# Column sums, mask loads and first small loads of the first product, in a two-block transformer kernel

## The chip, the cores and the metric

The kernel runs on one core of a Trainium2 chip. Times are device microseconds of one execution. The core's engines are TensorE (PE in the profile, its weight loads PEld), VectorE (DVE), ScalarE (ACT), GpSimd (POOL) and SyncE (SP, which issues nearly all DMAs here). Each engine takes its own instructions in order; an instruction waits for what it needs from the others.

## The reference

Two blocks of two layers each, for 256 rows of 1024 numbers, in float32. Only the start of the first layer matters here: an adaptive norm (adaLN), then the first product.

```python
def adaln_norm(x, c, g, w_ada, b_ada):
    mod = jax.nn.silu(c) @ w_ada + b_ada          # c: 1 x 1024, w_ada: 1024 x 3072
    shift, scale, gate = jnp.split(mod, 3, axis=-1)
    h = rms_norm(x, g) * (1.0 + scale[:, None, :]) + shift[:, None, :]
    return h, gate[:, None, :]

def nsa_mixer(h, w_in, pe_k, pe_v, ck_w1, ck_w2, cv_w1, cv_w2, w_out):
    u = h @ w_in                                   # the first product, 1024 x 2864
    ...                                            # q, k, v, z, gates are cut from u
    k_cmp = compress(k_c, pe_k, ck_w1, ck_w2)      # silu(blk @ w1) @ w2
    v_cmp = compress(v_c, pe_v, cv_w1, cv_w2)
    ...                                            # three attention branches, gated and projected
```

## The kernel before

Every large product is made in three matmuls of split float32 weights and activations: `make` (L199) loads one unit of a weight into one of five `wraw` buffers, ACT copies it to the high part (L210), and DVE subtracts to get the low part (L211). `pump` (L214) calls `make` as long as units are free. The five `wraw` buffers are shared by the weights of w_in and by those of adaLN.

The first product runs over the eight blocks k of 128 rows of w_in. For block k, `load` (L708) fetches the 128 shift and 128 scale columns of adaLN's weight, all 1024 rows, as two raw buffers `u` of four row blocks each, 1 MB in all, and two units of w_in (816 and 512 columns). `modulate(k)` (L720) forms, on 128 partitions, the sum over the eight row blocks r[j] times silu(c): ACT starts two accumulators ac (L725), DVE adds the other six row blocks in turn to one and to the other (L727), and PE sums each over the partitions against a column of ones (L731, L732; a float32 matmul is two instructions in the trace). From the sums come scale and shift (L734, L735), with which ACT makes block k of the normed input (L737, L740) and DVE its low part (L741). `multiply(k)` (L743) then adds block k to six accumulators in PSUM (L239, L240, L243). `modulate(k)` stands ahead of `multiply(k - 1)`, with a raised priority (`first(HEAD)`).

The order on each engine is set when the kernel is built, from priorities and from the order in which the program asks for things. After `modulate(7)` the program asks for the constants `cc` behind the last load so far, calls `pump` (the first four units of w_in's remaining 512 columns and two of the key compression's `nsa_ck_w1`), asks for the masks (`load_masks`, L159: two DMAs of 544 columns to 128 partitions into `wide` buffers, casts to bf16 on POOL), for the position table `peT` and the compression's second weights, and then for `multiply(7)`. Behind it come the copies of the product's results (`q_side`, `k_side`, `kvT`), the rope on DVE with its last addition on POOL (L440 to L442, L447), transposes on PE (L320), the rest of the product (`dense_cols`) and the compression (L839). `wide` has five buffers, taken in turn by xn, xn, m, m, then four q tiles (L810, filled at L812).

At the very start SP issues, in this order, the identity, the two halves of x, and three small columns `ccol`, `gcol`, `bcol` (8, 8 and 16 numbers to a partition), and then adaLN's first weights. [L127 to L137 below]

Of the kernel before, what the change touches and what calls it, by code (L numbers as in the profile page):

```python
# [8 lines left out]
F32 = mybir.dt.float32  # L9
F32R = mybir.dt.float32r  # L10
BF = mybir.dt.bfloat16
AF = mybir.ActivationFunctionType
ALU = mybir.AluOpType
# [81 lines left out]
def body(ctx: ExitStack, tc: tile.TileContext, A: dict, out: bass.AP, stop=None):  # L95
    nc = tc.nc
    pe, act, dve, pool = nc.tensor, nc.scalar, nc.vector, nc.gpsimd
# [8 lines left out]
    def nm(s):  # L106
        count[0] += 1
        return f"{s}{count[0]}"
# [11 lines left out]
    def ps(kind):  # L120
        b = banks[kind]
        i = turn.get(kind, 0)
        turn[kind] = i + 1
        return pp.tile([128, 512], F32, tag=f"b{b[i % len(b)]}", name=nm("ps"))


    ident = cp.tile([128, 128], F32, name="ident")  # L127
    nc.sync.dma_start(ident, A["k_ident"])
    x = [ap_.tile([128, D], F32, name=f"x{b}") for b in range(2)]
    for b in range(2):  # L130
        nc.sync.dma_start(x[b], A["x"][0, b * 128:(b + 1) * 128, :])
    ccol = cp.tile([128, 8], F32, name="ccol")
    nc.sync.dma_start(ccol, A["c_col"])
    gcol = cp.tile([128, 8], F32, name="gcol")
    nc.sync.dma_start(gcol, A["g_col"])
    bcol = cp.tile([128, 16], F32, name="bcol")
    nc.sync.dma_start(bcol, A["b_col"])  # L137
    ones = cp.tile([128, 128], F32, name="ones")
    dve.memset(ones, 1.0)
    nhalf = cp.tile([128, 1], F32, name="nhalf")  # L140
# [7 lines left out]
    def wide(name):  # L148
        return ap_.tile([128, D], F32, tag="bc", bufs=5, name=nm(name))
# [6 lines left out]
    def small(n=8):  # L156
        return ap_.tile([128, 12], F32, tag="sm", bufs=12, name=nm("sm"))[:, :n]

    def load_masks():  # L159
        for a, b in ((0, 544), (544, 1088)):  # L160
            m = wide("m")[:, :b - a]
            nc.sync.dma_start(m, A["k_mask"][:, a:b])
            if a == 0:
                pool.tensor_copy(mask[:, a:b], m)
            else:
                pool.tensor_copy(mask[:, a:1024], m[:, :1024 - a])
                pool.tensor_copy(mask[:, 1472:1536], m[:, 1024 - a:])
        pool.memset(mask[:, 1024:1152], 0.0)
        pool.tensor_copy(mask[:, 1152:1280], mask[:, 128:256])
        pool.memset(mask[:, 1280:1472], 0.0)  # L170

    def opened(name):
        cm = tc.tile_pool(name=name, bufs=1)
        return cm, cm.__enter__()

    def closed(cm):
        cm.__exit__(None, None, None)
# [3 lines left out]
    state = {"next": 0, "live": 0, "gate": None, "hold": False, "group": 2, "av": None}  # L181

    def behind(ins):
        return nullcontext() if ins is None else tc.issue_after(ins.ins)
# [29 lines left out]
    def pump():  # L214
        while not state["hold"] and len(made) < len(specs) and len(made) - (state["next"] - state["live"]) < NB:
            make()
# [11 lines left out]
    def mm3(p, xt, k, w, kw, c, start, stop):  # L228
        products(p, [(xt, k, w, kw)], c, start, stop)
# [107 lines left out]
    def rms_rstd(src, n, eps=1e-6):  # L337
        s = small(1)
        act.activation(junk[:, :n], src, AF.Square, accum_out=s)
        return rstd_of(s, 1.0 / n, eps)  # L340
# [278 lines left out]
    cs = cp.tile([128, 8], F32, name="cs")  # L619
# [77 lines left out]
    cmA, a0 = opened("ada0")  # L697
    xnT = a0.tile([128, 8, 256], F32, name="xnT")
    for tok in range(2):
        r = rms_rstd(x[tok], D)  # L700
# [19 lines left out]

    def modulate(k):
        r = raws[k]
        ac = [a0.tile([128, 256], F32, tag="aacc", bufs=4, name=nm("ac")) for _ in range(2)]
        for i in range(2):
            act.activation(ac[i], r[i], AF.Copy, scale=cs[:, i:i + 1])  # L725
        for j in range(2, 8):
            dve.scalar_tensor_tensor(ac[j % 2], r[j], cs[:, j:j + 1], ac[j % 2], op0=ALU.mult, op1=ALU.add)  # L727
        p = ps("pt")
        for i in range(2):
            c = slice(i * 128, (i + 1) * 128)  # L730
            pe.matmul(p[:, i:i + 1], lhsT=ac[0][:, c], rhs=ones[:, 0:1], start=True, stop=False)  # L731
            pe.matmul(p[:, i:i + 1], lhsT=ac[1][:, c], rhs=ones[:, 0:1], start=False, stop=True)  # L732
        ab = small(2)
        dve.scalar_tensor_tensor(ab[:, 1:2], p[:, 1:2], bcol[:, 8 + k:9 + k], gcol[:, k:k + 1], op0=ALU.add, op1=ALU.mult)  # L734
        dve.tensor_scalar(ab[:, 0:1], p[:, 0:1], bcol[:, k:k + 1], None, op0=ALU.add)  # L735
        hk = a0.tile([128, 256], F32, tag="hk", bufs=2, name=nm("hk"))
        act.activation(hk, xnT[:, k, :], AF.Identity, scale=ab[:, 1:2], bias=ab[:, 0:1])  # L737
        for tok in range(2):
            c = slice(tok * 128, (tok + 1) * 128)
            act.activation(xt[tok][0][:, k, :], hk[:, c], AF.Copy)  # L740
            dve.tensor_sub(xt[tok][1][:, k, :], hk[:, c], xt[tok][0][:, k, :].bitcast(F32))  # L741

    def multiply(k):  # L743
        state["next"] += 2
        w = made[state["next"] - 2:state["next"]]
        for gi, (i, c) in enumerate(((0, slice(0, 384)), (0, slice(384, 816)), (1, slice(0, 512)))):
            for tok in range(2):
                mm3(accp[gi * 2 + tok][:, :c.stop - c.start], xt[tok], k, w[i], 0, c, k == 0, k == 7)

    load(0)  # L750
    for k in range(8):
        if k < 7:
            load(k + 1)
        else:
            make()
            make()
        with first(HEAD):
            modulate(k)
        if k:
            multiply(k - 1)  # L760
# [1 line left out]
    with behind(state["dma"]):  # L762
        nc.sync.dma_start(cc, A["k_cc"])
    pump()
    load_masks()
    nc.sync.dma_start(peT, A["pe_T"])
    for j in range(2):
        nc.sync.dma_start(w2k[:, :, j * 64:(j + 1) * 64], A["nsa_ck_w2"][0].rearrange("(k p) n -> p k n", p=128))
    nc.sync.dma_start(w2v, A["nsa_cv_w2"][0].rearrange("(k p) n -> p k n", p=128))
    multiply(7)  # L770
    closed(cmA)


# [4 lines left out]
    with first(ATTN):  # L778
        pool.tensor_copy(cmask, cc[:, C_CADD:C_CADD + 2 * NCMP].rearrange("p (t n) -> p t n", t=2))
        for tok in range(2):  # L780
            dup = pK.tile([128, 4, 2, 64], F32, tag="kvd", bufs=2, name=nm("kvd"))
            act.activation(dup, accp[tok][:, :256].rearrange("p (a d) -> p a d", a=4)[:, :, None, :].to_broadcast([128, 4, 2, 64]), AF.Copy)
            p = ps("pt")
# [33 lines left out]
    with first(SINK):  # L817
        for tok in range(2):
            q_side(tok, 1, accp[4 + tok])
        for tok in range(2):  # L820
            k_side(accp[tok], tok, 256, 384, 0)
            p = accp[2 + tok]
# [30 lines left out]
    p = ps("c")  # L853
# [9 lines left out]
    for g in range(2):  # L863
        p = ps("c")
# [120 lines left out]
    with tc.tile_pool(name="dil", bufs=1) as dp:  # L985
# [42 lines left out]
        with first(ATTN):  # L1028
# [8 lines left out]
            for tok in range(2):  # L1037
# [10 lines left out]
                for i, (a, b) in enumerate(((0, 6), (6, 8))):  # L1048
                    c = slice(a * 64, b * 64)
# [118 lines left out]
    with tc.tile_pool(name="ab", bufs=1) as bp:  # L1168
# [74 lines left out]
        with first(ATTN):  # L1243
            o = [ps("o"), ps("o")]
            dve.tensor_scalar(nsink, sinks, -1.0, None, op0=ALU.mult)
            for h in range(8):
# [5 lines left out]
                if h % 2:  # L1252
                    c = slice(h - 1, h + 1)
# [153 lines left out]
```

## Time and profile before

| | us |
|---|---|
| median of 3 runs | 997.05 |
| lowest and highest | 995.78, 997.25 |
| the profiled execution's own time | 994.04 |
| its span, first to last instruction | 992.3 |
| PE busy in it | 934.9 (94%) |
| DVE busy | 701.5 (71%) |
| ACT busy | 538.8 (54%) |
| POOL busy | 40.6 (4%) |
| DMA, mean over the span | 179 GB/s |
| mean granted TensorE clock | 0.983 |

The shares are means over some thousand microseconds, most of which are feed-forward products. The first 80 us look different, and the change lies there. A timeline row gives the start, the length, the engine, the line and the operation; in brackets stands how long the engine sat idle before it, and what released it. A row of several instructions (x2) gives the time from the first one's start to the last one's end.

### The profile page before, as it was taken

The page shows a single profiled execution, that of the slowest core. Times are in us where ns is not written, and L with a number is a line of the kernel's source. Part 1 is how long each engine was busy: PE and PEld are TensorE (multiplying, and loading weights), DVE is VectorE, ACT ScalarE, POOL GpSimd, SP SyncE. Part 2 cuts the span into 40 slices and gives each one's busy share as a digit, 9 for nine tenths or more (in the row PEclk, how much of TensorE's full clock was granted, in tenths as well). Part 3 has the DMA queues.
Part 4 walks back from the last instruction along what each step waited for, and adds up shares of the span by engine and source line. Part 5 has one row for each costly group of instructions (what it writes and reads, how often), then busy time and mean ns, then how long its engine had stood idle before and what let it go on. Part 6 is the DMA issues. An engine that isn't in the chain of part 4 may idle for free.

```text
span 992.3 us, 14766 instructions
## 1 busy us (share of the span) xinstructions
PE 934.9 (94%) x5316; PEld 783.7 (79%) x5316; DVE 701.5 (71%) x1454; ACT 538.8 (54%) x1062; POOL 40.6 (4%) x49
## 2 busy tenths in 40 slices
PE   5997998899999998999799999999999899999996
PEld 4876786687778877967788888887997688888885
DVE  5888899858777768586857565677466676665655
ACT  5584567834545626486346554435676355555540
POOL 1003000001120001000000000000000000000000
PEclk9998798999999999999999999999999999999999
DMA  9996787334855425632356554655635243565541
GB/s 288 304 311 217 221 269 253 108 106 151 261 202 182 149 66 197 236 111 86 95 203 212 170 184 159 241 181 151 221 132 152 90 167 126 193 235 170 182 137 43
DMA packets 106169, 177.66 MB, mean 179 GB/s; under 512 B 8816, under 2 KB 40688, under 8 KB 106096
## 3 DMA queue, kind: packets, MB, share of 16 engines
q1 hardware_dynamic: 106096, 176.72, 54.6%
q8 instruction: 42, 0.69, 0.3%
q14 instruction: 31, 0.25, 0.1%
HBM read 175.65 MB, written 1.05 MB: 178 GB/s over the span
## 4 chain that ended last, share of the span: by engine, by line
PE 77%; DVE 11%; ACT 5%; DMA 4%; issue 2%; SPq 1%; POOL 0%; DVEq 0%; ACTq 0%; POOLq 0%
PE ps L279 15%; PE ps L239 13%; PE ps L240 13%; PE ps L243 13%; PE ps L280 8%; DVE wl L211 2%; DMA wr<-in_ada_w_dram 2%; PE ps L469 2%; PE ps L320 1%; DVE ac L660 1%; PE ps L839 1%; PE ps L525 1%; ACT e L482 1%; PE ps L297 1%; PE ps L298 1%
## 5 line engine op out<-in xcount | busy, mean ns | idle before, releaser
L211 DVE TENSOR_TENSOR wl<-wr,wh 128x1024 fp32r<-128x1024 f32 (+5 forms) x276 | 319.6, 1195 | 78.7 <-ACT wh L210 77.3
L210 ACT ACTIVATE wh<-wr 128x1024 fp32r<-128x1024 f32 (+5 forms) x276 | 270.6, 1021 | 72.4 <-PE ps L243 21.2
L279 PE MATMUL ps<-xhl,wh 128*128 128x512 f32 x640 | 226.5, 398 | 0.0
L239 PE MATMUL ps<-wh,xhl 128*128 128x512 f32 (+5 forms) x544 | 197.4, 375 | 4.5 <-ACT xhl L312 2.4
L240 PE MATMUL ps<-wl,xhl 128*128 128x512 f32 (+5 forms) x544 | 199.0, 368 | 0.0
L280 PE MATMUL ps<-xhl,wl 128*128 128x256 f32 x640 | 179.2, 281 | 0.0
L243 PE MATMUL ps<-wh,xhl 128*128 128x512 f32 (+5 forms) x544 | 172.9, 370 | 0.9 <-DVE xhl L313 0.6
L279 PEld LDWEIGHTS ps<-xhl,wh 128*128 128x128 f32 x640 | 120.0, 188 | 28.9
L280 PEld LDWEIGHTS ps<-xhl,wl 128*128 128x128 f32 x640 | 120.9, 189 | 1.1
L239 PEld LDWEIGHTS ps<-wh,xhl 128*128 128x128 f32 x544 | 103.6, 192 | 22.8 <-ACT xhl L312 5.1
L240 PEld LDWEIGHTS ps<-wl,xhl 128*128 128x128 f32 x544 | 104.5, 192 | 14.0 <-issue 0.2
L243 PEld LDWEIGHTS ps<-wh,xhl 128*128 128x128 f32 x544 | 99.8, 190 | 18.2 <-DVE xhl L313 2.4
L1124 ACT ACTIVATE hs<-ps 128x256 f32<-128x256 f32 x80 | 30.0, 377 | 100.1 <-PE ps L280 100.1
L1125 DVE TENSOR_TENSOR hs<-ps,hs 128x256 f32<-128x256 f32 x80 | 32.6, 420 | 68.4 <-ACT hs L1124 68.4
L243 PE MATMUL ps<-wh,hl 128*128 128x512 f32 x176 | 68.3, 390 | 0.0
L240 PE MATMUL ps<-wl,hh 128*128 128x512 f32 x176 | 68.3, 390 | 0.0
L239 PE MATMUL ps<-wh,hh 128*128 128x512 f32 x176 | 66.7, 390 | 0.0
L482 ACT ACTIVATE e<-e,sm 128x128 f32<-128x128 f32 x112 | 49.6, 445 | 12.7 <-DVE sm L476 12.6
L312 ACT ACTIVATE xhl<-ps 128x512 fp32r<-128x512 f32 x28 | 16.5, 597 | 67.9 <-PE ps L309 67.8
L476 DVE CUSTOM_DVE_ANT_0 e<-ps,mask 128x128 f32<-128x128 f32 (+1 forms) x144 | 44.1, 350 | 8.8 <-PE ps L489 4.3
L660 DVE SCALAR_TENSOR_TENSOR ac<-ar,cs,ac 128x512 f32<-128x512 f32 x56 | 42.7, 764 | 4.0 <-DMA ar<-in_ada_w_dram 3.7
L334 POOL TENSOR_TENSOR sm<-sm,nhalf 128x1 f32<-128x1 f32 x18 | 13.2, 734 | 721.3 <-DVE sm L333 721.3
(315 smaller groups left out, 1299.3 us busy)
## 6 DMA issues: line engine op xcount, KB each, us to landing
wr<-in_ffn_w_gate_dram SPq DMA_DIRECT2D x44, 512.0 KB, 4.7
wr<-in_ffn_w_up_dram SPq DMA_DIRECT2D x44, 512.0 KB, 4.7
wr<-in_ffn_w_down_dram SPq DMA_DIRECT2D x44, 512.0 KB, 5.0
ar<-in_ada_w_dram SPq DMA_DIRECT2D x32, 512.0 KB, 4.5
wr<-in_dil_w_in_dram SPq DMA_DIRECT2D x32, 512.0 KB, 4.6
wr<-in_cd_w_in_dram SPq DMA_DIRECT2D x22, 512.0 KB, 4.4
wr<-in_ada_w_dram SPq DMA_DIRECT2D x32, 256.0 KB, 4.9
wr<-in_nsa_w_in_dram SPq DMA_DIRECT2D x12, 512.0 KB, 5.0
```

The costliest lines, as they stand in the source:

```text
L210: act.activation(hi, raw[:, :nk * n], AF.Copy)
L211: dve.tensor_sub(lo, raw[:, :nk * n], hi.bitcast(F32))
L239: pe.matmul(p, lhsT=xt[0][:, k, :], rhs=w[0][:, kw, c], start=start and t == 0, stop=False)
L240: pe.matmul(p, lhsT=xt[0][:, k, :], rhs=w[1][:, kw, c], start=False, stop=False)
L243: pe.matmul(p, lhsT=xt[1][:, k, :], rhs=w[0][:, kw, c], start=False, stop=stop and t == n - 1)
L279: pe.matmul(p, lhsT=w[0], rhs=xhl[:, k].rearrange("p a t -> p (a t)"), start=k == 0, stop=False)
L280: pe.matmul(p[:, :256], lhsT=w[1], rhs=xh[:, k, :], start=False, stop=k == 7)
L476: state["dve"] = dve.tensor_tensor_reduce(out=e[:, c0:c1], in0=s[:, c0:c1], in1=added[:, 256 - (c1 - c0):], scale=-scale, scalar=3e38, op0 ...
L482: act.activation(e[:, c0:c1], e[:, c0:c1], AF.Exp, bias=n2[:, i:i + 1], scale=-1.0, accum_out=den[:, i:i + 1])
L660: dve.scalar_tensor_tensor(ac, raw[:, j, :], cs[:, k:k + 1], ac, op0=ALU.mult, op1=ALU.add)
L1124: act.activation(t[:, c], p[:, 256:], AF.Copy)
L1125: dve.tensor_add(t[:, c], p[:, :256], t[:, c])
```

## The change

Four edits. The identity and the three columns are issued from ACT's queue and no longer from SP's. `modulate` has one accumulator: ACT starts it with r[0], DVE adds seven row blocks one after the other into the same tile, and PE makes one sum over partitions for each of the two columns, where it made two. `load_masks` moves from ahead of `peT` and the small weights to behind `multiply(7)`, and it is bound to come behind the last weight load that `pump` has asked for, the second unit of `nsa_ck_w1`.

```diff
     ident = cp.tile([128, 128], F32, name="ident")
-    nc.sync.dma_start(ident, A["k_ident"])
+    nc.scalar.dma_start(ident, A["k_ident"])
...
-    nc.sync.dma_start(ccol, A["c_col"])
+    nc.scalar.dma_start(ccol, A["c_col"])
...
-    nc.sync.dma_start(gcol, A["g_col"])
+    nc.scalar.dma_start(gcol, A["g_col"])
...
-    nc.sync.dma_start(bcol, A["b_col"])
+    nc.scalar.dma_start(bcol, A["b_col"])
...
     def modulate(k):
         r = raws[k]
-        ac = [a0.tile([128, 256], F32, tag="aacc", bufs=4, name=nm("ac")) for _ in range(2)]
-        for i in range(2):
-            act.activation(ac[i], r[i], AF.Copy, scale=cs[:, i:i + 1])
-        for j in range(2, 8):
-            dve.scalar_tensor_tensor(ac[j % 2], r[j], cs[:, j:j + 1], ac[j % 2], op0=ALU.mult, op1=ALU.add)
+        ac = a0.tile([128, 256], F32, tag="aacc", bufs=4, name=nm("ac"))
+        act.activation(ac, r[0], AF.Copy, scale=cs[:, 0:1])
+        for j in range(1, 8):
+            dve.scalar_tensor_tensor(ac, r[j], cs[:, j:j + 1], ac, op0=ALU.mult, op1=ALU.add)
         p = ps("pt")
         for i in range(2):
             c = slice(i * 128, (i + 1) * 128)
-            pe.matmul(p[:, i:i + 1], lhsT=ac[0][:, c], rhs=ones[:, 0:1], start=True, stop=False)
-            pe.matmul(p[:, i:i + 1], lhsT=ac[1][:, c], rhs=ones[:, 0:1], start=False, stop=True)
+            pe.matmul(p[:, i:i + 1], lhsT=ac[:, c], rhs=ones[:, 0:1], start=True, stop=True)
...
     pump()
-    load_masks()
     nc.sync.dma_start(peT, A["pe_T"])
...
     multiply(7)
+    with behind(state["dma"]):
+        load_masks()
     closed(cmA)
```

## Rows read from the trace of the kernel before

**Rows 1.** Busy time by stretch: stretch, length, busy us (instructions), granted clock, DMA share, GB/s
```profile
9.69:19.14 9.45, 6.55 (x30) 5.69 (x28) 8.43 (x20) 5.76 (x11) 2.25 (x4) 1.00 1.07 312
19.14:52.28 33.14, 30.32 (x150) 26.49 (x150) 27.55 (x73) 19.67 (x43) 0.00 (x0) 1.00 1.04 312
9.69:52.28 42.59, 36.87 (x179) 32.18 (x177) 35.99 (x91) 25.43 (x53) 2.25 (x4) 1.00 1.05 312
```
**Rows 2.** The same view behind the first product (PE, PEld, DVE, ACT, POOL in turn)
```profile
59.65:73.50 13.85, 13.85 (x68) 11.00 (x67) 12.55 (x15) 13.53 (x21) 0.00 (x0) 1.00 0.94 291
73.50:79.70 6.20, 0.07 (x1) 0.00 (x0) 6.20 (x14) 3.77 (x7) 1.30 (x1) 0.91 0.95 332
79.70:90.00 10.30, 10.29 (x63) 8.88 (x64) 10.30 (x22) 4.52 (x7) 3.54 (x2) 0.73 0.59 199
```
**Rows 3.** Timeline of the first 10 us: SP's issues, and ACT's first work
```profile
0.73 0.39 SPq L128 DMA_DIRECT2D ident<-in_k_ident_dram  x1
1.17 0.89 SPq L131 DMA_DIRECT2D x<-in_x_dram  x2
...
3.57 6.14 SPq L713 DMA_DIRECT2D wr<-in_ada_w_dram  x8
4.86 1.06 ACT L339 ACTIVATE junk<-x 128x1024 bf16<-128x1024 f32 x1 [2.85 <-DMA x<-in_x_dram]
```
**Rows 4.** DMA throughput in 40 slices: of 11 to 19 us, then of 50 to 76
```profile
GB/s 294 300 302 282 289 297 333 320 338 361 343 324 413 355 331 403 353 401 408 411 381 421 339 326 315 208 153 192 187 242 253 320 245 236 328 333 351 312 323 302
...
GB/s 363 385 372 394 384 300 294 375 328 337 161 195 372 384 425 370 370 372 373 343 306 356 232 39 331 356 150 178 345 336 326 284 236 381 266 140 301 362 370 362
```
**Rows 5.** DVE timeline: additions to two accumulators in turn, then to one
```profile
49.00 0.89 DVE L727 SCALAR_TENSOR_TENSOR ac<-wr,cs,ac 128x256 f32<-128x256 f32 x2 [0.66 <-ACT ac L725]
...
51.18 0.48 DVE L727 SCALAR_TENSOR_TENSOR ac<-wr,cs,ac 128x256 f32<-128x256 f32 x1
51.58 0.28 DVE L741 TENSOR_TENSOR xhl<-hk,xhl 128x128 fp32r<-128x128 f32 x1
51.78 0.48 DVE L727 SCALAR_TENSOR_TENSOR ac<-wr,cs,ac 128x256 f32<-128x256 f32 x1
...
131.50 0.75 DVE L660 SCALAR_TENSOR_TENSOR ac<-ar,cs,ac 128x512 f32<-128x512 f32 x1
...
133.67 1.53 DVE L660 SCALAR_TENSOR_TENSOR ac<-ar,cs,ac 128x512 f32<-128x512 f32 x2
```
**Rows 6.** DVE groups by form, 9.69 to 52.28: count, busy, mean ns, idle before
```profile
L727 DVE SCALAR_TENSOR_TENSOR ac<-wr,cs,ac 128x256 f32<-128x256 f32 x48 | 21.3, 480 | 5.7 <-ACT ac L725 4.2 <-DMA wr<-in_ada_w_dram 1.2
```
**Rows 7.** PE timeline at the last block: sums over partitions, then the product
```profile
52.31 0.38 PE L732 MATMUL ps<-ones,ac 128*128 128x1 f32 x2 [0.22 <-DVE ac L727]
...
53.00 1.44 PE L239 MATMUL ps<-wh,xhl 128*128 128x384 f32 x6
```
**Rows 8.** Timeline behind the first product, of SP, ACT, DVE, POOL and PE
```profile
55.74 8.22 SPq L205 DMA_DIRECT2D wr<-in_nsa_ck_w_dram  x4
...
72.86 1.06 ACT L210 ACTIVATE wh<-wr 128x1024 fp32r<-128x1024 f32 x1 [0.19 <-DMA wr<-in_nsa_cv_w_dram]
...
76.84 0.67 DVE L440 TENSOR_TENSOR rt<-q,cc 128x512 f32<-128x512 f32 x1
...
78.36 1.30 POOL L447 TENSOR_TENSOR q<-rt,rt 128x512 f32<-128x512 f32 x1 [23.20 <-DVE rt L442]
...
79.71 1.11 PE L320 MATMUL ps<-ident,q 128*128 128x128 f32 x4 [6.14 <-POOL q L447]
```
**Rows 9.** DVE's subtractions beside work on POOL and without it; one group by form
```profile
16.55 1.11 DVE L211 TENSOR_TENSOR wl<-wr,wh 128x816 fp32r<-128x816 f32 x1 [0.27 <-ACT wh L210]
...
L211 DVE TENSOR_TENSOR wl<-wr,wh 128x816 fp32r<-128x816 f32 x6 | 6.0, 1008 | 1.8 <-ACT wh L210 1.8
...
72.87 1.21 DVE L211 TENSOR_TENSOR wl<-wr,wh 128x1024 fp32r<-128x1024 f32 x1
...
79.04 1.70 DVE L211 TENSOR_TENSOR wl<-wr,wh 128x1024 fp32r<-128x1024 f32 x1
```

## The prediction

> **What bounds the kernel now.** The page's shares say PE, but they are means; all four edits act before 80 us, so I read the busy time by stretch first. From 9.69 us, where DVE begins the first column sum, to 52.28, where it ends the last, the DMA engines are never free (share 1.05, 312 GB/s) and DVE is busy for 35.99 of 42.59 us [rows 1]. So the first product runs at the pace of its loads, and DVE is the next limit, with 6.6 us of idle time spread over eight blocks. PE's figure of 36.87 is no limit: it waits for the sums. Behind the product the limit changes: from 59.65 to 73.50 ACT is busy for 13.53 of 13.85 us and DVE for 12.55, and then DVE for all of 6.20 us, while PE stands still [rows 2]. PE's 6.14 us of idle time are released by POOL's rope addition, which waited for DVE's rope at 76.84, which stood behind the weights of the compression [rows 8]. From there on PE is the bound, so what moves 79.71 moves the end by about as much.
>
> **The change part by part.**
>
> *Small loads from ACT.* SP's first issue of x moves from 1.17 to 0.73 us [rows 3]: 0.4 us sooner for a queue that is then full. The bytes stay. ACT's four issues, at 0.4 us each, lie in the 2.85 us in which it waits for x [rows 3]; without that cover they would cost 1.7 us. SP's issue time that is saved (four, 1.8 us) brings nothing more as long as the engines and not the issues limit the loads: the first eight loads of adaLN take 6.14 us to issue, 0.77 apart, which is the pace at which 256 KB pass at some 340 GB/s.
>
> *Masks out of the way.* Two loads of 544 x 4 x 128 bytes, 0.56 MB. Where they pass, at 13 to 15 us, the queue moves about 400 GB/s [rows 4], so the loads behind them come 1.4 us sooner. At 312 GB/s it would be 1.8. I take 1.4; with the 0.4 the loads of the first product lead by 1.8 us.
>
> *One chain on DVE.* Per block one addition more, seven for six. The price of one changes as well. Today neighbours write different accumulators and start 0.40 us apart, though each lasts 0.48: two take 0.89 [rows 5]. No pair of 256 columns on one accumulator is in the trace, but one of 512 is: two take 1.53 where one takes 0.75 [rows 5], so the second starts 0.03 behind the end of the first. For 256 columns that is 0.51 us from start to start. The lower bound is today's 0.40. In the second half of a block, two short subtractions (L741) stand between the additions, and these start 0.60 apart already [rows 5], so the dependence is hidden there except at the first pair (0.11). The first half grows from two additions at 0.40 to three at 0.51, 0.75 us more. Together 0.87 us per block, 7.0 us over eight; with everything hidden, 0.4 a block and 3.2 us. I take 7.0, since the row is of the same operation.
>
> That is against 6.6 us of idle time. DVE would need 35.99 + 7.0 = 43.0 us; begun 0.4 us sooner, at 9.25, it ends at 52.25 if it never waits. It waited for 5.7 us at these additions [rows 6]; as the loads lead by up to 1.8 us most of that goes, and I leave 0.3. The last sum is then ready at 52.5, 0.2 later than now, and the lead of the loads is used up. DVE has become the limit. A later DVE also frees the five raw buffers later; I count nothing for it, as the loads then have 1.8 us in hand.
>
> The Trainium skill, page "VectorE: DVE Perf Modes", section "The DRAIN you can't avoid", says that the next operation starts only when the pipe is empty and that a semaphore between two costs nothing extra. By that rule a chain would cost no more per addition than two accumulators. The trace does not agree: 0.40 us apart at a length of 0.48 in the one case, 0.78 at 0.75 in the other [rows 5]. What would follow from it stands under the first rival.
>
> *ACT and the sums.* ACT loses one of two activations per block. It has idle time (19.67 of 33.14 us [rows 1]): 0. On PE, three pairs follow the last addition today, 52.31 to 53.00, 0.23 each [rows 7]; two are left, so 0.2 us is gained at the last block. At the other blocks PE waits anyway: 0.
>
> Product: +0.2 - 0.2 = 0.
>
> *Masks behind the compression's weights.* They are asked for behind the second unit of `nsa_ck_w1`. Queued behind them on SP are the third and fourth and the value weights. SP's two more issues (0.9 us) fit between those four, which stretch over 8.22 us as they wait for buffers [rows 8]. In the queue the masks push the units behind them by 1.4 us. The queue has holes near 57, 65 and 67 us (slices of 161, 39 and 150 GB/s among some of 350 [rows 4]), which give most of it back before the value weights, whose wait on ACT is only 0.19 us today [rows 8]. But ACT is 98% busy and in order, so a late unit delays the copies queued behind it. Bounds 0 and 1.4; I take 0.3, near the low end for the holes. The wide buffers do not bind: the last q tile takes the first mask's buffer at about 75 us, when its cast is long done. POOL's next work behind the casts is the rope addition at 78.36, after 23.20 us of idle time [rows 8].
>
> *The casts.* 2.25 us of POOL [rows 1] move from 16 us, where they are not seen, to some 66 us, where DVE is full. Beside them a subtraction took 1.11 us, against 1.008 [rows 9]; beside a rope addition of 1.30 us on POOL one took 1.70, against 1.21 [rows 9]. By the first row two such subtractions lose 0.2 us, by the second 2.25 x 0.49 / 1.30 = 0.85. I take 0.2, the row of the casts themselves. The Trainium skill, page "SBUF — State Buffer", section "SBUF: two separate sides", has GpSimd and a DVE operation with two SBUF inputs lock each other out entirely; that would add up to 2.25 us. The subtraction beside the casts lost 0.10, far less.
>
> Sum: 0 + 0.3 + 0.2 = +0.5 us at 79.7 and at the end. The profiled execution took 994.04 us (span 992.3, 1.7 around it), 3.0 less than the median, so 994.5 there and **997.5** as a median: no change that shows, as about 0.2%, 2 us, is what a measurement of this kernel can tell from none.
>
> **The rivals.**
>
> *The loads keep the pace (faster).* If the built order puts other DVE work between the additions, the chain costs 3.2 us, which fit into 6.6. The product then ends 1.8 + 0.2 = 2.0 us sooner; behind it, with the masks in the queue's holes and the casts at 0.1, -1.9 remains: 995.1. With 1.8 us for the masks, -2.3. For it: the second halves are already interleaved. Against it: the rows of the chain. (The rule of the Trainium skill's page "VectorE: DVE Perf Modes", section "The DRAIN you can't avoid", would bring the same outcome.)
>
> *The hole on PE closes (faster).* The 6.14 us in which PE waits for the rope are a matter of order: PE's queue has the transposes ahead of the compression's matmuls. The granted clock is 0.73 in the 10.3 us behind the hole, so part of it ran at 1.2 GHz [rows 2]. If later weights let the rope pass ahead on DVE by two subtractions of 1.21 us, PE resumes 2.4 us sooner, and a clock that falls less gives back some 1.6 of the 10.3 x 0.27 = 2.8 us lost there: -4, 993.0. Nothing in the trace says that the order will change so.
>
> *Late weights (slower).* If the masks delay the third compression unit by the full 1.4 us, ACT, in order, passes it on to the rope and PE's hole grows by that much; the casts at 0.85 and 1.0 us of waits on DVE in the first product in place of 0.3 bring +2.95: 1000.0. It decides from the point at which DVE has no idle time left in the first product, for then the loads' lead does not exist when the masks enter. For it: DVE at 99% by the sum above. Against it: the holes in the queue.
>
> *It does not do what it says:* if the masks still go out early or the issue slot of x does not move, 0 to 1 us is lost or gained; that lies within the forecast.
>
> **How the numbers follow.** Forecast 0.42, of which 0.36 within 2 us, 0.02 faster and 0.04 slower; loads keep the pace 0.24 (0.15 faster, 0.09 same, as it lies at the edge); hole closes 0.12; late weights 0.22 (0.20 slower, 0.02 same). So faster 0.29, same 0.47, slower 0.24. The range goes from 993.6, which leaves out half of the hole's case, to 1000.4, which takes in the slower one to a little over its time.
>
> **What would show it.** One chain: additions 0.51 us apart, DVE without idle time from 19 to 52 us, the last sum within 0.7 us of 52.3. If DVE still has 3 us idle there and the last sum is ready before 51.2, the first rival holds. The masks' casts near 66 us, and the rope near 77.3; PE's hole of 6 us still there, the clock still low behind it. If the hole is shorter by 2 us or longer by 1, the order or the weights decided and not the sums. I would be wrong in kind if the time went by more than 2 us with the rope within 1 us of where it is: the change would then act behind 80 us, where I count nothing.

## The result and the profile after

| | before | after |
|---|---|---|
| median of the runs shown together, us | 997.15 (995.78 to 998.19) | 1008.62 (1004.42 to 1013.91) |
| profiled execution, us (span) | 994.04 (992.3) | 1008.35 (1006.3) |
| mean granted TensorE clock | 0.983 | 0.971 |

The changed kernel is slower: the ratio of the times is 1.0105, with a 95% interval of 1.0072 to 1.0137 (it is formed otherwise than as the quotient of the two medians, and can differ from that; so can the ratios below). The prediction of 997.5 us, and its range up to 1000.4, missed it. In the changed kernel's file the additions stand in line 726, the sums in 730, AB (scale and shift, the two small operations behind the sums) in 732 and 733, hk in 735, the split of the normed block in 738 and 739, and the copies of the product's results in 781.

First the busy time by stretch, over the stretches of [rows 1, 2]:

```profile
9.69:19.14 9.45, 3.78 (x17) 2.71 (x16) 7.96 (x18) 3.90 (x7) 0.00 (x0) 0.82 0.99 258
19.14:52.28 33.14, 24.72 (x104) 21.93 (x105) 26.37 (x67) 14.98 (x32) 0.00 (x0) 0.81 0.92 270
59.65:73.50 13.85, 8.76 (x39) 7.65 (x38) 8.39 (x13) 8.51 (x13) 2.22 (x5) 0.88 0.99 336
79.70:90.00 10.30, 7.22 (x39) 5.75 (x38) 9.38 (x19) 7.62 (x13) 1.29 (x1) 1.00 0.67 231
```

I had expected VectorE without idle time here. From 19.14 to 52.28 us it is busy for 26.37 us, less than before (27.55), and so are ScalarE (14.98 against 19.67) and TensorE (24.72 against 30.32). The loads run at 270 GB/s, no longer at 312. When all four are less busy than before, no engine has become the bound; they wait for each other. The waits from 19 to 72 us name whom (waiting engine and line, releaser, total us, times, longest):

```profile
ACT wh L210 <- DMA wr<-in_nsa_w_in_dram: 17.2, 9, 4.4
PE ps L239 <- ACT xhl L738: 9.4, 3, 4.9
DVE wl L211 <- ACT wh L210: 8.9, 6, 3.2
```

One turn of this ring, block by block in the timeline of the changed kernel:

```profile
39.08 1.27 DVE L726 SCALAR_TENSOR_TENSOR ac<-wr,cs,ac 128x256 f32<-128x256 f32 x3
41.83 0.50 PE L730 MATMUL ps<-ones,ac 128*128 128x1 f32 x4
42.61 1.40 ACT L210 ACTIVATE wh<-wr 128x816 fp32r<-128x816 f32 x2 [4.38 <-DMA wr<-in_nsa_w_in_dram]
43.53 1.01 DVE L211 TENSOR_TENSOR wl<-wr,wh 128x816 fp32r<-128x816 f32 x1 [3.19 <-ACT wh L210]
44.56 1.33 SPq L205 DMA_DIRECT2D wr<-in_nsa_w_in_dram  x3
45.85 0.21 DVE L732 SCALAR_TENSOR_TENSOR sm<-ps,bcol,gcol 128x1 f32<-128x1 f32 x1
46.22 0.60 ACT L735 ACTIVATE hk<-xnT,sm 128x256 f32<-128x256 f32 x1 [0.85 <-DVE sm L733]
47.21 0.69 PE L239 MATMUL ps<-wh,xhl 128*128 128x384 f32 x1 [4.88 <-ACT xhl L738]
...
71.05 0.60 ACT L781 ACTIVATE kvd<-ps 128x512 f32<-128x512 f32 x1 [2.05 <-PE ps L243]
...
86.08 0.68 DVE L440 TENSOR_TENSOR rt<-q,cc 128x512 f32<-128x512 f32 x1
88.95 0.66 PE L320 MATMUL ps<-ident,q 128*128 128x128 f32 x4 [3.08 <-POOL q L447]
```

TensorE has its sums through soon after 41.83 us. But VectorE, next in its queue, holds a weight's low part, which waits 3.19 us for ScalarE, which waits 4.38 us for a load. The two small operations that turn the sums into scale and shift stand behind it, at 45.85; the norm follows at 46.22, and TensorE, after 4.88 us of idle time, at 47.21. SP can ask for the next weights only at 44.56, when a raw buffer is free again, so the next load is late as well. The granted clock is 0.81 over the stretch, a mixture of its levels of 1.2 and 2.4 GHz, where it was 1.00. The copy of the product's results stands at 71.05 us, where it stood at 59.65: **11.4 us late**; how much of that reaches the end of the execution is taken up under what stays open. The rope follows 9.2 us late (86.08 against 76.84 [rows 8]), TensorE goes on 9.2 us late, after 3.08 us of idle time and not 6.14, and its clock does not fall behind that (1.00, where it was 0.73 [rows 2]).

What put a weight ahead of the scale? The order of the instructions on the engines. The change does not ask for it, yet the built kernel has another one. Below, a4 is an addition (on ScalarE the start of a column sum) of block 4, S4 the sums over partitions, AB4 scale and shift, hk4 the norm, x4 its split, wh4 and wl4 the weights' high and low parts (two units, a and b), M4 the 18 products:

```
before  ScalarE  a5 a5 hk4 x4 x4 wh4a wh4b
        VectorE  AB4 a5 a5 a5 a5 x4 a5 x4 a5 wl4a wl4b
        TensorE  S4 M3 S5 M4 S6 M5 S7 M6 M7
after   ScalarE  a6 hk4 x4 x4 wh5a wh5b
        VectorE  a5 wl4a a5 wl4b a5 AB4 a5 a6 a5 a6 x4 x4 a6 a6 a6 wl5a a6 AB5 wl5b
        TensorE  M3 S4 M4(6) S5 M4(12) S6 M5 M6 S7 M7
```

Before, the sums of block k+1 precede the products of block k, the norm of block k precedes its weights on ScalarE, and a block's additions stand together. After, weights are taken in one block ahead of the norm, their low parts and the next block's additions stand among a block's last additions, and four of the six sums in the steady part stand within or behind the products that they preceded.

### The profile page after: what moved, and what is told of

Read it like the earlier page. It is cut to its first block, busy times and chain, and to the rows that moved or that the text cites. A ratio compares the mean times of both kernels' runs of the same rounds, so it can differ in the third digit from the quotient of the medians.

```text
span 1006.3 us, 14705 instructions
## 1 busy us (share of the span) xinstructions
PE 934.4 (93%) x5284; PEld 783.4 (78%) x5284; DVE 704.4 (70%) x1462; ACT 535.6 (53%) x1054; POOL 38.2 (4%) x49
## 3 DMA queue, kind: packets, MB, share of 16 engines
HBM read 175.65 MB, written 1.05 MB: 176 GB/s over the span
## 4 chain that ended last, share of the span: by engine, by line
PE 78%; DVE 9%; ACT 5%; DMA 5%; issue 2%; SPq 0%; POOL 0%; DVEq 0%; ACTq 0%; POOLq 0%
PE ps L279 15%; PE ps L239 14%; PE ps L240 13%; PE ps L243 13%; PE ps L280 8%; DMA wr<-in_nsa_w_in_dram 3%; PE ps L469 2%; ACT wh L210 2%; DVE wl L211 1%; PE ps L320 1%; ACT e L482 1%; PE ps L309 1%; PE ps L525 1%; PE ps L297 1%; PE ps L298 1%
## 5 line engine op out<-in xcount | busy, mean ns | idle before, releaser
L239 PE MATMUL ps<-wh,xhl 128*128 128x512 f32 (+4 forms) x544 | 205.1, 381 | 13.7 <-ACT xhl L738 9.4
L240 PE MATMUL ps<-wl,xhl 128*128 128x512 f32 (+5 forms) x544 | 202.5, 375 | 0.0
L243 PE MATMUL ps<-wh,xhl 128*128 128x512 f32 (+5 forms) x544 | 169.1, 372 | 0.9 <-DVE xhl L313 0.6
L239 PEld LDWEIGHTS ps<-wh,xhl 128*128 128x128 f32 x544 | 106.8, 196 | 32.4 <-ACT xhl L738 10.0
L240 PEld LDWEIGHTS ps<-wl,xhl 128*128 128x128 f32 x544 | 106.9, 197 | 13.8 <-issue 0.2
L243 PEld LDWEIGHTS ps<-wh,xhl 128*128 128x128 f32 x544 | 101.0, 193 | 19.0 <-issue 2.5
```

The costliest lines, as they stand in the source:

```text
L239: pe.matmul(p, lhsT=xt[0][:, k, :], rhs=w[0][:, kw, c], start=start and t == 0, stop=False)
L240: pe.matmul(p, lhsT=xt[0][:, k, :], rhs=w[1][:, kw, c], start=False, stop=False)
L243: pe.matmul(p, lhsT=xt[1][:, k, :], rhs=w[0][:, kw, c], start=False, stop=stop and t == n - 1)
```

## Experiments

Unless the diff says otherwise, each is the kernel before with one edit. "Product ends" is the start of the first copy of its results on ScalarE, 59.65 us before and 71.05 after. That copy can also wait for what stands ahead of it on ScalarE; where this matters, the end of TensorE's last six products is given beside it. The bounds of a ratio are its 95% interval; the times of the kernel before in the three sets were 998.0, 998.1 and 998.75 us.

**1. All but the chain (e1): the changed kernel with the two accumulators put back.**

```diff
-        ac = a0.tile([128, 256], F32, tag="aacc", bufs=4, name=nm("ac"))
-        act.activation(ac, r[0], AF.Copy, scale=cs[:, 0:1])
+        ac = [a0.tile([128, 256], F32, tag="aacc", bufs=4, name=nm("ac")) for _ in range(2)]
+        for i in range(2):
+            act.activation(ac[i], r[i], AF.Copy, scale=cs[:, i:i + 1])
...
```

> The changed kernel with the two accumulators and four sums of before put back; masks behind the compression's weights and small loads from ScalarE stay. Theory A (order: on one accumulator each addition waits for the one ahead, so the built order puts the weights' subtractions and the next block's additions between the last additions of a block, and the sums wait for later loads): the loss goes, 994 to 998 us against 997.15 of before, product end near 58 us. Theory B (length: the chain is simply 7 us more DVE work): the same, 994 to 998. Theory C (masks and small loads make the loss, by shared queue slots and late weights): 1005 to 1009 stays.

Measured: 1001.0 us, ratio 1.0019 (0.9997 to 1.0042); the product ends at 59.00. Masks and small loads are not what costs 11 us. The time lies above the 994 to 998 us that A and B expected. The built order is not that of before here either: ScalarE has `wh2a wh2b a4 a4 hk2 x2 x2 hk3 wh3a x3 x3 wh3b`, and on TensorE the sums of blocks 2 and 4 lie in part within products. So these edits alone turn the order too, though in this form it costs the product nothing.

**2. The chain alone (e2): the second edit of the change, nothing else.**

```diff
-            dve.scalar_tensor_tensor(ac[j % 2], r[j], cs[:, j:j + 1], ac[j % 2], op0=ALU.mult, op1=ALU.add)
+            dve.scalar_tensor_tensor(ac, r[j], cs[:, j:j + 1], ac, op0=ALU.mult, op1=ALU.add)
...
-            pe.matmul(p[:, i:i + 1], lhsT=ac[0][:, c], rhs=ones[:, 0:1], start=True, stop=False)
-            pe.matmul(p[:, i:i + 1], lhsT=ac[1][:, c], rhs=ones[:, 0:1], start=False, stop=True)
+            pe.matmul(p[:, i:i + 1], lhsT=ac[:, c], rhs=ones[:, 0:1], start=True, stop=True)
```

> The kernel before with one accumulator, seven additions in a chain and one sum per column, nothing else of the change. A and B: 1005 to 1011 us, the end of the first product near 70 us where it was 59.65. C: 996 to 999.

Measured: 1011.6 us, ratio 1.0134 (1.0095 to 1.0173); the product ends at 70.14. The whole loss comes with this edit. Its built order is akin to that of the changed kernel but not the same (TensorE has `S4 M3 M4 S5 M5(6) S6 M5(12) S7 M6 M7`).

**3. Seven operations on VectorE, but two accumulators (e3).**

```diff
-        for i in range(2):
-            act.activation(ac[i], r[i], AF.Copy, scale=cs[:, i:i + 1])
+        act.activation(ac[0], r[0], AF.Copy, scale=cs[:, 0:1])
+        dve.tensor_scalar(ac[1], r[1], cs[:, 1:2], None, op0=ALU.mult)
```

> The kernel before with the second accumulator started on VectorE in place of ScalarE: seven VectorE operations per block as in the change, but in two chains. A (order, from the dependence): the additions stay together, some 0.4 us per block more VectorE work hide in its 6.6 us of idle time, 996.5 to 999 us. B (length): 3.2 us more work, so at least a part of it shows, 998 to 1001 us. If the number of operations alone breaks the order: 1005 or more.

Measured: 997.5 us, ratio 1.0006 (0.9984 to 1.0028); the product ends at 59.50. The built order is that of before but for small shifts: on TensorE four products lie within the sums of each of the blocks 4 to 7, and on VectorE some additions stand ahead of AB. The seventh operation is shorter than an addition (0.35 us), but its number alone does no harm. What changes the order in e2 is in the one accumulator or in its two sums.

**4. The chain, with VectorE's additions kept together (e4).** The low parts are asked for behind a block's last addition, and a block's first addition is bound behind the last one of the block before.

```diff
+            with behind(state["sum"]) if j == 1 else nullcontext():
+                ins = dve.scalar_tensor_tensor(ac, r[j], cs[:, j:j + 1], ac, op0=ALU.mult, op1=ALU.add)
+        state["sum"] = ins
...
+        with behind(state["sum"]):
+            for low in todo:
+                low()
```

> As the chain alone, but the low-part subtractions of a block's weights are asked for behind the last addition of the next block, and a block's first addition is bound behind the last one of the block ahead: the order of before, with the length of the chain. A: the length itself is 0.87 us per block against 6.6 us of idle time, so 997 to 1001 us, with the product's end within 2.5 us of 59.65. B: the loss stays, 1005 to 1010 us.

Measured: 1010.4 us, ratio 1.014 (1.011 to 1.017); the product ends at 73.28. Taken at its word this speaks against the order (A there) and for the chain's length (B). But I had bound one engine of three. The waits of this kernel from 9 to 62 us show what moved in its place:

```profile
PEld ps L242 <- ACT xhl L743: 7.9, 4, 2.8
ACT hk L740 <- DVE sm L738: 6.1, 4, 2.8
```

ScalarE now had `hk4 wh4b x4`, a weight between the norm and its split, and TensorE had the sums within the products. So the run decides nothing, and the next four bind all three engines. There the order is theory O, the chain's own length theory L.

**5. The chain in the order of before (e5).** Every instruction of the first product on ScalarE (A), VectorE (V) and TensorE (P) is asked for in one written order and bound behind the last one on its engine. With two accumulators this binding gives the three engines the order of the kernel before, instruction for instruction up to the product's end (e12 below), so it changes nothing there.

```diff
+    def put(e, f, *args, **kw):
+        with behind(state["pe"] if e == "P" else last[e]):
+            ins = f(*args, **kw)
...
+    ORDER = ("A:a0 V:a0 A:a1 V:a0 A:wh0a V:a0 A:wh0b V:a0*4 P:S0 V:a1*7 P:S1 V:wl0a V:AB0 A:hk0 ..."
...
+              "V:wl3b P:M3*18 V:AB4 A:hk4 V:a5 A:x4 V:a5 A:x4 V:a5 A:wh4a V:a5 A:wh4b V:a5 A:a6 V:x4 V:a5 V:x4 V:a5 P:S5 "
```

> The kernel before with the one chain and half the sums over partitions alone (as in the run with the chain only), but now with every instruction of the first product on ScalarE, VectorE and TensorE bound to the order that the kernel before has: the sums of block k+1 ahead of the products of block k on TensorE, the norm of block k ahead of the high parts of weights k on ScalarE, a block's additions together on VectorE. Theory O (the order on the three engines carries the loss, the chain's own length hides): the first product ends at 59.5 to 62 us and the time is 995 to 1001 us. Theory L (the eight longer rows of dependent additions themselves are too much for VectorE): the product ends at 67 us or later and the time is 1005 to 1013 us, as with the chain alone.

Measured: 999.0 us, ratio **1.0004** (0.9986 to 1.0022). The loss is gone, with the same chain and the same two sums. The product ends at 63.12, 3.5 us later than before and 1 us behind what O allowed. Timeline of this kernel, where all bound instructions have the helper's line 726:

```profile
50.39 2.56 DVE L726 SCALAR_TENSOR_TENSOR ac<-wr,cs,ac 128x256 f32<-128x256 f32 x5
...
53.67 0.48 DVE L726 SCALAR_TENSOR_TENSOR ac<-wr,cs,ac 128x256 f32<-128x256 f32 x1
...
60.95 1.35 PE L790 MATMUL ps<-wh,xhl 128*128 128x384 f32 x6
...
62.16 1.06 ACT L210 ACTIVATE wh<-wr 128x1024 fp32r<-128x1024 f32 x1 [0.28 <-PE ps L790]
63.12 0.58 ACT L860 ACTIVATE kvd<-ps 128x512 f32<-128x512 f32 x1
...
79.62 0.69 DVE L440 TENSOR_TENSOR rt<-q,cc 128x512 f32<-128x512 f32 x1
82.51 1.12 PE L320 MATMUL ps<-ident,q 128*128 128x128 f32 x4 [5.50 <-POOL q L447]
```

Five additions in a row take 2.56 us, so they start (2.56 - 0.48) / 4 = 0.52 us apart, and the last one ends at 54.15 us, 1.9 later than before. That is what the chain itself costs: TensorE's last six products begin 1.9 us later too (60.95 against 59.10), and the rest of the copy's 3.5 us is one more weight ahead of it on ScalarE (62.16). TensorE resumes 2.8 us later than before (79.71 [rows 8]); at 170 us the lag is 0.3 us.

**6. The reverse: two accumulators in the order of the changed kernel (e6).** Here and in e9 to e11 the diff shows the order in the notation above, not lines of the file.

```diff
-    TensorE  S4 M3 S5 M4 S6 M5 S7 M6 M7
+    TensorE  M3 S4 M4(6) S5 M4(12) S6 M5 M6 S7 M7
...
-    ScalarE  a5 a5 hk4 x4 x4 wh4a wh4b
+    ScalarE  a6 a6 hk4 x4 x4 wh5a wh5b
```

> The reverse: the kernel before with its two accumulators, six additions and four sums per block, masks and small loads where they were, but the first product bound to the order of the changed kernel on ScalarE, VectorE and TensorE (sums of a block behind the products of the block before it, high parts of weights one block ahead of the norm, low parts and the next block's additions among a block's last additions). Theory O: the product ends at 67 to 73 us and the time is 1004 to 1013 us, as in the changed kernel. Theory L: the order is harmless, the product ends at 59 to 62 us and the time is 995 to 1000 us.

Measured: 1005.5 us, ratio **1.0074** (1.0045 to 1.0104); the product ends at 73.53. The kernel before loses this with nothing changed but the order, and TensorE waits as in the changed kernel:

```profile
PE ps L791 <- ACT xhl L726: 7.2, 4, 4.3
```

Together, over the kernel before: the whole change in the order of before (e7 below) +0.04%, the order of the changed kernel alone +0.74%, the two together (the changed kernel) +1.05%. The 0.3% by which the last is more than the two before it is no more than their intervals leave open.

**7. The whole change in the order of before (e7).** The diff is that of the change and of e5.

> The whole change (one chain, half the sums, masks behind the compression's weights, first small loads from ScalarE), with the first product bound to the order of the kernel before on the three engines. Theory O: the product ends at 58 to 61 us (the masks' 0.5 MB is out of the way) and the time is 992 to 999 us, so the change as such is worth -4 to +2 us. Theory L: the product ends at 66 us or later and the time is 1004 to 1012 us.

Measured: 998.2 us, ratio 1.0004 (0.9979 to 1.0028); the product ends at 61.54, the last addition at 52.74. Given the old order, the change neither gains nor loses. The product's end lies 0.5 us behind what O allowed. The granted clock is 0.91 here from 19 to 53 us (the row stands further below), so a clock below 1.00 there does not bring the loss by itself.

**8. Masks and small loads alone, in the order of before (e8).** The kernel of e1 with e5's binding.

> The masks and the small loads as in the change, the two accumulators as before, and the first product bound to the order of the kernel before. Theory O: the product ends 1 to 3 us sooner than before (56.5 to 58.7 us) and the time is 993 to 998 us. A rival, that the late masks or ScalarE's loads cost something of their own behind the product (their run without the bound order was 1001.0 us against 998.0): 999 to 1003 us in spite of a product that ends sooner.

Measured: 996.6 us, ratio 0.9983 (0.9962 to 1.0004); the product ends at 58.27, 1.4 us sooner (TensorE's last products, at 58.67, 1.8 us sooner). The same instructions in the order that was built for them took 1001.0 us (e1), but there TensorE's last products ended at 58.2 us, so what e1 loses against e8 does not lie in the first product.

Which engine's order is it? Two accumulators again, with the changed kernel's order on some engines and that of before on the others.

**9. TensorE's order alone (e9).**

```diff
-    TensorE  S4 M3 S5 M4 S6 M5 S7 M6 M7
+    TensorE  M3 S4 M4(6) S5 M4(12) S6 M5 M6 S7 M7
```

> The kernel before with two accumulators, the first product bound to before's order on ScalarE and VectorE, and to the changed kernel's order on TensorE alone: from block 3 on the sums over partitions of block k+1 stand behind most or all of the products of block k. Theory P (the late sums are what costs: the norm of a block begins only when the products of the block before it are through, and TensorE stands idle for it): the product ends at 66 to 74 us and the time is 1002 to 1010 us. Theory S (the order on ScalarE and VectorE costs, weights ahead of what the products wait for): the product ends at 59.5 to 63 us and the time is 996 to 1001 us.

**10. ScalarE's order alone (e10).**

```diff
-    ScalarE  a5 a5 hk4 x4 x4 wh4a wh4b
+    ScalarE  a6 a6 hk4 x4 x4 wh5a wh5b
```

> The same with the changed kernel's order on ScalarE alone (the high parts of weights k+1 and the start of block k+2's column sum ahead of the norm of block k+1), before's order on VectorE and TensorE. Theory P: the product ends at 59.5 to 64 us and the time is 996 to 1002 us. Theory S: the norm of a block waits behind a weight that has not landed; the product ends at 66 to 74 us and the time is 1002 to 1010 us.

**11. ScalarE's and VectorE's order (e11).**

```diff
-    VectorE  AB4 a5 a5 a5 a5 x4 a5 x4 a5 wl4a wl4b
+    VectorE  a5 wl4a a5 wl4b a5 AB4 a5 a6 a5 x4 x4 a6 a6 a6 wl5a a6 AB5 wl5b
...
```

> The changed kernel's order on ScalarE and on VectorE (the low parts of weights and the next block's additions among a block's last additions), before's order on TensorE, so that the sums stand ahead of the products again; two accumulators. Theory P: the product ends at 59.5 to 65 us and the time is 996 to 1003 us, the two others' order being cheap as long as the sums come early. Theory S: the product ends at 68 to 76 us and the time is 1004 to 1012 us, as with all three orders (73.5 us and 1005.5 us).

| | us | ratio | product ends, us |
|---|---|---|---|
| e9 TensorE | 1005.1 | 1.0070 (1.0048 to 1.0091) | 71.62 |
| e10 ScalarE | 1024.0 | 1.0225 (1.0186 to 1.0264) | 82.10 |
| e11 ScalarE and VectorE | 1006.3 | 1.0065 (1.0040 to 1.0091) | 71.90 |

P holds in e9, S in e11, and e10 goes far beyond S: both engines' orders cost, each in its own way, and a mixture can cost more than all three together. The waits from 19 to 72 us, e9, then e10, then e11:

```profile
DVE sm L726 <- PE ps L726: 11.1, 5, 3.5
ACT hk L726 <- DVE sm L726: 10.8, 5, 3.7
PE ps L791 <- ACT xhl L726: 5.4, 2, 4.5
```

```profile
ACT wh L726 <- DMA wr<-in_nsa_w_in_dram: 26.8, 9, 5.4
DVE xhl L726 <- ACT xhl L726: 25.7, 6, 5.8
PE ps L726 <- DVE ac L726: 13.5, 7, 4.5
```

```profile
ACT wh L726 <- DMA wr<-in_nsa_w_in_dram: 10.4, 8, 2.4
PE ps L726 <- DVE ac L726: 8.4, 8, 2.1
DVE wl L726 <- ACT wh L726: 6.5, 7, 1.6
```

In e9 the chain of small steps from the sums to the split starts when TensorE has multiplied, not while it multiplies, so VectorE waits for TensorE and ScalarE for VectorE. In e10 ScalarE waits for a weight with the norm behind it, and VectorE for that norm's split, with additions and low parts behind it that would set raw buffers free for the next weight. Timeline of e10, one turn:

```profile
30.57 1.41 ACT L726 ACTIVATE wh<-wr 128x816 fp32r<-128x816 f32 x2 [4.50 <-DMA wr<-in_nsa_w_in_dram]
...
35.78 0.29 DVE L726 TENSOR_TENSOR xhl<-hk,xhl 128x128 fp32r<-128x128 f32 x1 [5.02 <-ACT xhl L726]
35.99 0.48 DVE L726 SCALAR_TENSOR_TENSOR ac<-wr,cs,ac 128x256 f32<-128x256 f32 x1
...
36.49 1.49 SPq L738 DMA_DIRECT2D wr<-in_nsa_w_in_dram  x3
...
41.37 1.40 ACT L726 ACTIVATE wh<-wr 128x816 fp32r<-128x816 f32 x2 [5.42 <-DMA wr<-in_nsa_w_in_dram]
```

The addition that begins at 35.99, behind the split, ends at 36.47; SP asks for the next weights at 36.49; ScalarE has them at 41.37, and the norm behind them is late again. A VectorE order that fits ScalarE's (e11) takes most of that away.

**12. The late masks alone, in the order of before (e12).** The kernel of e8 with the first small loads on SP.

```diff
-    nc.scalar.dma_start(ident, A["k_ident"])
+    nc.sync.dma_start(ident, A["k_ident"])
...
```

> The late masks alone: two accumulators, before's order on the three engines in the first product, the first small loads on SyncE as before. If the masks are what ends the product sooner (it ended 1.4 us sooner with the masks and ScalarE's loads together), it ends at 57.8 to 58.6 us and the time is 993 to 998 us, as in that run (996.6 us). If ScalarE's loads brought that lead, it ends at 59.3 us or later and the time is that of before.

Measured: 996.8 us, ratio 0.9979 (0.9952 to 1.0006); the product ends at 59.62. By the product's end the lead would belong to ScalarE's loads, by the time the masks alone do as well as both. The profiled execution does not decide it: its x came at 6.04 us, where the kernel before has 4.86, so that it began 1.2 us behind; even so TensorE's last products end 0.2 us sooner than before, at 60.28. Timeline, ScalarE's first work:

```profile
6.04 1.06 ACT L339 ACTIVATE junk<-x 128x1024 bf16<-128x1024 f32 x1 [4.03 <-DMA x<-in_x_dram]
```

With ScalarE's issues x does come sooner: that first work starts at 4.56 to 4.76 us in the four kernels that have them (the changed kernel, e1, e7 and e8) and at 4.83 to 6.04 in the ten others. VectorE's first addition does not follow as clearly (8.92 to 9.21 us against 8.47 to 10.26), and that the time gains by it is not shown. e8 and e12 are the best of all versions, by 0.2%, and both intervals still reach 1.

## Why the prediction was wrong

**The step that failed** is the one on which the whole sum rested without saying so: that VectorE, ScalarE and TensorE take their instructions in the order of before. It lies under "I count nothing for it" for the buffers that are set free later and under "At the other blocks PE waits anyway: 0": in the new order late buffers and late sums are what costs. The order alone, with the old instructions, costs 0.74% (e6), the change in the order of before 0.04% (e7), both together 1.05%. The first rival did think of another built order, but as a gain: other work between the additions would hide the dependence. It came so, and the work was a subtraction that waited for a load.

**Loads and masks.** The sum had the loads 1.8 us ahead. With both edits in the old order the last addition ends 1.8 us sooner (50.48 us in e8 against 52.26) and TensorE's last products 1.8 us sooner, the copy 1.4 us; and with the chain 1.6 us sooner than without (63.12 to 61.54, e5 and e7). How it splits into 0.4 and 1.4 stays open.

**The chain on VectorE.** The 0.51 us from start to start was right (0.52 in e5). From the first addition to the end of the last VectorE is busy for 41.3 us in e5 and was for 36.0 before, so the chain's 7.0 us measured 5.3. The sum had the last addition done at 52.5 us, with the loads' lead; in e7 it is done at 52.74. But two terms of that were off and cancel. VectorE in e7, by stretch, and its additions from 9 to 60 us:

```profile
9.00:19.00 10.00, 4.82 (x24) 3.69 (x22) 9.64 (x22) 4.96 (x8) 0.00 (x0) 0.81 1.16 300
19.00:53.00 34.00, 28.25 (x130) 24.35 (x130) 31.28 (x78) 17.90 (x38) 0.00 (x0) 0.91 0.99 294
```

```profile
L726 DVE SCALAR_TENSOR_TENSOR ac<-wr,cs,ac 128x256 f32<-128x256 f32 x56 | 27.0, 483 | 3.6 <-ACT ac L726 2.3
```

It is busy for 9.64 + 31.28 = 40.9 of 44 us and not for 43.0 of 43.3, and it waits for 3.6 us at the additions and not for 0.3. The Trainium skill's page "VectorE: DVE Perf Modes", section "The DRAIN you can't avoid", says that a semaphore between two operations costs nothing extra, by which the starts would be as far apart as with two accumulators; e5's row does not agree, 0.52 us against 0.40. The same section of the Trainium skill also says that an operation that is not held starts earlier, which the prediction left out; the 0.40 us at a length of 0.48 [rows 5] agree with that.

**From the last addition to the product's end.** Here the forecast had -0.2, one pair of sums less, and so it came: from the end of the last addition to the end of TensorE's last six products it took 8.19 us before, 8.02 in e7 and 8.15 in e5. TensorE waits for the sums for longer at the earlier blocks (5.1 us in e5 from 19 to 72 us, 1.7 before), but that adds nothing at the end: "At the other blocks PE waits anyway: 0" held in the old order. That the copy is 1.9 us late in e7, and TensorE's last products only 0.3, comes from ScalarE, which has one more weight's high part ahead of it. The rows are first before, then e7:

```profile
58.68 1.06 ACT L210 ACTIVATE wh<-wr 128x1024 fp32r<-128x1024 f32 x1 [1.26 <-DMA wr<-in_nsa_w_in_dram]
59.10 1.35 PE L243 MATMUL ps<-wh,xhl 128*128 128x384 f32 x6
59.65 0.58 ACT L782 ACTIVATE kvd<-ps 128x512 f32<-128x512 f32 x1
...
59.39 1.37 PE L790 MATMUL ps<-wh,xhl 128*128 128x384 f32 x6
60.58 1.06 ACT L210 ACTIVATE wh<-wr 128x1024 fp32r<-128x1024 f32 x1 [0.26 <-PE ps L790]
61.54 0.58 ACT L861 ACTIVATE kvd<-ps 128x512 f32<-128x512 f32 x1
```

**Behind the product.** Masks and casts at +0.5: e7 resumes on TensorE at 80.15 us, 0.4 later than before, with last products that ended 0.3 later, so only 0.1 arose there. The forecast's +0.5 us at 79.7 thus nearly came, but not by its terms: it had 0 for the product and 0.5 behind it.

**The whole.** In the order of before the change costs 0.04% (-0.21 to +0.28), where the forecast said +0.5 us, 0.05%. That is close, in part by luck: two terms of the chain cancel, and the 0.4 us at 79.7 lay elsewhere than forecast. Above all it is the sum of a kernel that was not built.

**The rivals.** "The hole on PE closes" came true in part, the idle time fell from 6.14 to 3.08 us and the clock behind it stayed at 1.00, but it gave back some 2 of 11.4 us. "Late weights" had the right sign, and a late load that an engine working in order passes on, but put it behind the product, where the masks are; it lay within the product. Its condition, a VectorE without idle time there, did not come: VectorE was busy for 26.37 of 33.14 us. Two of the named signs did show it. The hole on PE became 3.06 us shorter, which was to say that "the order or the weights decided and not the sums"; and the rope was 9.2 us late, so the loss does not begin behind 80 us.

**What stays open.** Which property of the chain makes the builder turn the order in this way was not separated: the one accumulator and its two sums came together in the changed kernel, e2 and e4. Nor are they the only edit that turns it (e1). And the lag at the product's end is not the lag at the end of the execution; the prediction's "what moves 79.71 moves the end by about as much" does not hold for these executions. Measured as the median shift of ScalarE's instructions against the kernel before, the lag at the copy, then from 100 to 130 us, then at the end is +11.4, +7.5, +14.0 in the changed kernel, +3.5, +2.9, +2.3 in e5, and 0, +0.1, +2.7 in e12. The clearest case is e1: 2.8 us ahead of the kernel before from 100 to 130 us, 8.4 us behind it at the end. Steps of 1 to 5 us come in the attention stages (near 170 to 200, 480 and 800 us) with dips of the granted clock: from 790 to 830 us it was 0.96 before and 0.91 after. The order of instructions differs there too, and no run here separates it from chance. So of the 14.0 us in the changed kernel's profiled execution, 7.5 come through from the product, and the 6.5 that arise behind it are not explained. A part of them is the choice of executions: the medians differ by 11.5 us, the profiled execution of before was 3 us quicker than its median, and executions of that kernel alone ran from 993.8 us at a granted clock of 0.980 to 1005.3 us at 0.964.

## What to carry to other kernels

An edit that makes one step longer or more dependent, or one that only moves loads (e1), can turn the order in which all engines take their work, where that order is made by a builder. So compare the built orders of the two kernels around the change before the durations are summed, and if they differ, price the new order: look for an instruction that waits for a late load with something urgent behind it. A different order is not yet a loss: e1's cost the product nothing. To try a small edit fairly, bind its surroundings to the old order on every engine that takes part; to bind one of three only moves the wait.

## What was not expected of the hardware

In e8, one of the masks' casts on POOL, 64 columns wide, took 10.32 us, while VectorE was busy for all of those 10.32 us. In the changed kernel the same cast took 0.24 us, with VectorE idle throughout.

```profile
67.11 10.32 POOL L167 CAST mask<-m 128x64 bf16<-128x64 f32 x1
...
77.25 0.27 DVE L440 TENSOR_TENSOR rt<-ps,cc 128x128 f32<-128x128 f32 x1
...
77.63 1.28 POOL L447 TENSOR_TENSOR q<-rt,rt 128x512 f32<-128x512 f32 x1
```

I had priced the casts as a loss to VectorE; here POOL seems to have waited for VectorE. From 67.23 us VectorE's operations had two inputs from SBUF each; the cast ended at 77.43, 0.18 us after the first one with an input from PSUM had begun (77.25). The profile's page says that spans on POOL are rough, but POOL's next work did start only at 77.37 us. The Trainium skill, page "SBUF — State Buffer", section "SBUF: two separate sides", has one of GpSimd and a VectorE operation with two SBUF inputs block the other for as long as it runs; that agrees with this row. It cost 0.3 us at most there: the rope addition that stands behind the casts on POOL, at 77.63, needs VectorE's rope, which was done at 77.33 us.
